# Float32r matmuls that read their tile and write their bank from the last column to the first

## The chip, the core and the metric

The kernel runs on one core of a Trainium2 chip. The metric is the device time of one execution in microseconds. The core's engines work side by side and meet at semaphores: TensorE (PE in the profile, its weight loads PEld), VectorE (DVE), ScalarE (ACT), GpSimd (POOL) and SyncE (SP, which issues most DMAs). A matmul takes a stationary operand of 128x128 and streams a moving operand of up to 512 columns past it; the product lands in one of eight banks of PSUM, with 128 rows of 512 float32 columns each.

## What is computed

One decoder layer on 256 tokens of width 2048, all in float32:

```python
h = rmsnorm(x, norm_attn_pre)
proj = h @ w_in                       # 2048 -> 4160: q, k, v of A, and c_q, c_kv, k_r of B
a_out = dilated window attention of A # 8 heads x 128, three windows merged
c_q, c_kv = rmsnorm(c_q), rmsnorm(c_kv)
q_b = c_q @ w_uq                      # 512 -> 8 x 192
kv = c_kv @ w_ukv                     # 512 -> 8 x 256
b_out = causal attention of B         # 8 heads
x = x + rmsnorm(concat(a_out, b_out) @ w_out)   # 2048 -> 2048
h = rmsnorm(x, norm_mlp_pre)
u = square(relu(h @ w_up))            # 2048 -> 8192
x = x + rmsnorm(u @ w_down)           # 8192 -> 2048
```

## The kernel before

The large products are made with float32r operands, a form of float32 that TensorE streams faster than float32 itself and rounds. To keep the precision, every operand is split in two float32r parts, `hi` (the rounded value, made by ScalarE at L306 or L310) and `lo` (what is left, made by VectorE at L307 or L311), and a product is the sum of three matmuls: hi x hi, hi x lo, lo x hi. The activations, transposed, are the stationary operand, 128 tokens at a time (`tok`), and the weights are the moving one, mostly 512 columns at a time. Of the weights' 1024-column tiles `hi` and `lo` there are eight buffers each; they are loaded on SP's queue, and partly on POOL's.

All float32r matmuls but the last 48 are issued by the helper `mm` (L295, the matmul itself is L296 in the profile); it issues the float32 matmuls of the attention too. The last 48, of the final group of `w_down`, are issued in `three_more` (L1188). Transposes are float32 and have a helper of their own (L300). The callers of `mm` are `proj` (the projections `w_in`, `w_ukv`, `w_uq` and `w_out`; its tiles have 512, 288 or 384 columns), `three` (L1016: the three matmuls of one product, used for `w_up` and `w_down`, 512 columns) and the attention heads. In `w_up` and `w_down` some blocks are multiplied with seven products in place of eight, in the manner of Strassen (`seven_products`, L1021); sums of weights and of activations are made for that on VectorE, and products are gathered in further banks (`m`, `md`).

The order of the work is written by hand. A small clock (`Flow`) in the building program adds an assumed time for each matmul, and chains of other work (evacuations, softmax, norms) are put between the matmuls when that clock says that they are due. The framework then adds the semaphores: an instruction waits for whatever wrote what it reads, or still reads what it overwrites, and also TensorE for itself, where a bank gets a new use.

Of the kernel before, what the change touches and what calls it, by code (L numbers as in the profile page):

```python
# [19 lines left out]
F32R = mybir.dt.float32r  # L20
# [243 lines left out]
def layer(nc, tc, io):  # L264
# [28 lines left out]


    def mm(out, a, b, start, stop, cost=MM):  # L295
        nc.tensor.matmul(out, a, b, start=start, stop=stop)  # L296
        flow.spend(cost)

# [160 lines left out]
    def proj(aT, chs, name, order=None, need=None, bank_of=None):  # L459
# [6 lines left out]
        for c, t, b in order:  # L466
            ch = chs[c]
            i, k0, kp = ch.tiles[t]
            ws = [weights.get(x) for x in (i if isinstance(i, list) else [i])]
            i = i if isinstance(i, list) else [i]  # L470
            if need:
                need(k0 + kp - 1, b)
            if i[0] < FINE:
                hl = [(0, 0), (1, 0)], [(0, 1)]
            else:
                hl = [(0, 0), (0, 1), (1, 0)],
            for g, passes in enumerate(hl):
                for kk in range(kp):
                    k = k0 + kk
                    for j, (o, m) in enumerate(ch.cuts):  # L480
                        wt, o = (ws[j], 0) if len(ws) > 1 else (ws[0], o)
                        for p, (x, w) in enumerate(passes):
                            mm(accs[c][b][j][:, :m], tok(aT[x], k, b), wt[w][:, kk, o:o + m],
                               k == 0 and g == 0 and p == 0,
                               k == ch.nk - 1 and g == len(hl) - 1 and p == len(passes) - 1, MM * m / 512)
                    flow.pump()
            left[c, b] -= 1
            for x in i:
                uses[x] = uses.get(x, 0) + 1
                if uses[x] == NB:  # L490
                    weights.free(x)
            if not left[c, b]:
                yield c, b, accs[c][b]
# [121 lines left out]
    def softmax_pv(wk, dl, sc, bias, scale, v, head, name):  # L615

        s = wk.tile([P, 384], F32, tag="s", bufs=2, name=f"s_{name}")
        st = wk.tile([P, 8], F32, tag="st", bufs=3, name=f"st_{name}")
        spans = ((0, 128, bias[:, 128:256]), (128, 384, bias))
        for i, (a, e, m) in enumerate(spans):  # L620
            nc.vector.tensor_tensor_reduce(
                out=s[:, a:e], in0=sc[:, a:e], in1=m, op0=OP.add, op1=OP.max, scale=1.0,
                scalar=-3e38, accum_out=st[:, i:i + 1])
        nc.vector.tensor_scalar_mul(st[:, 2:4], st[:, 0:2], -scale)
        yield dl[2]
        for i, (a, e, m) in enumerate(spans):
            nc.scalar.activation(s[:, a:e], s[:, a:e], AF.Exp, bias=st[:, 2 + i:3 + i], scale=scale,
                                 accum_out=st[:, 4 + i:5 + i])
        yield dl[3]
        nc.vector.reciprocal(st[:, 6:8], st[:, 4:6])  # L630
        for i, (a, e, m) in enumerate(spans):
            nc.vector.tensor_scalar_mul(s[:, a:e], s[:, a:e], st[:, 6 + i:7 + i])
        yield dl[4]
        tp = tp_bank(f"pT_{name}")
        for c in range(3):
            transpose(tp[:, c * P:(c + 1) * P], s[:, c * P:(c + 1) * P])
        pT = wk.tile([P, 384], F32, tag="pT", bufs=2, name=f"pT_{name}")
        nc.scalar.activation(pT, tp[:, :384], AF.Copy)
        yield dl[5]
        o = at_bank(f"o_{name}")  # L640
        mm(o[:, :S], v[0], pT[:, :S], True, False, 2 * MM)
        mm(o[:, P:S], v[1], pT[:, S:384], False, True, MM)
        split(mixT[0][:, head, :], mixT[1][:, head, :], o[:, :S])
# [407 lines left out]
    for j in range(FF // CW):  # L1051
# [9 lines left out]
        for t, b in order:  # L1061
# [19 lines left out]
            if what == "k":  # L1081
                w = weights.get(tiles[0])
# [102 lines left out]
    def three_more(out, a, w):  # L1185

        for x, z in ((0, 0), (0, 1), (1, 0)):
            nc.tensor.matmul(out, a[x], w[z], start=False, stop=(x, z) == (1, 0), skip_group_check=True)  # L1188
            flow.spend(MM)

    hp.release()
# [5 lines left out]
    for c in range(2):  # L1197
# [5 lines left out]
        for t, (what, k, tiles) in enumerate(wide_d[c]):  # L1203
# [4 lines left out]
            if what == "k":  # L1208
                w = weights.get(tiles[0])
# [37 lines left out]
    for g in (GT - 2, GT - 1):  # L1247
        for b, n in PARTS:
            for kk in range(4):
                k = 4 * g + kk  # L1250
                w = weights.get(tail[k])
                if g < GT - 1:
                    down_mm(1, us[1, g], k, b, n, w, False, kk == 3)
                else:
                    three_more(y[b][2 + n], [tok(us[1, g][x], kk, b) for x in range(2)],
                               [t[:, 0, n * 512:n * 512 + 512] for t in w])
                if (b, n) == PARTS[-1]:
                    weights.free(tail[k])
                flow.pump()
            if g < GT - 1:  # L1260
                nc.vector.tensor_tensor(out=y[b][2 + n], in0=y[b][2 + n], in1=more[b, n], op=OP.add)
                if (b, n) == (0, 0):
                    us[1, g + 1] = split_u(1, g + 1)
            elif n == 0:
                square(2, b)
                gain(2, b)
            else:
                fin = flow.start(final(b))
# [40 lines left out]
```

## Time and profile before

| | |
|---|---|
| median of 3 runs | 1047.4 us (1047.33 to 1047.88) |
| profiled execution, first to last instruction (span) | 1045.7 us |
| TensorE busy | 1035.7 us, 99% |
| VectorE, ScalarE, GpSimd busy | 80%, 60%, 5% |
| mean granted clock of TensorE | 0.997 |
| DMA | 229 MB, 219 GB/s over the span |

The profile gives the span of the execution that it took and no time of its own beside it; the median of the unprofiled runs is 1.7 us longer than this span. A busy time is the sum over an engine's instructions with overlaps counted once. Matmuls overlap in the pipeline, so a matmul's duration in a row is longer than the distance to the next one's start; that distance is read from the timeline, or from the chain that ended last, which names stretches of equal matmuls with start, length and count. In rows, `y<-hi,uhi` is output<-moving operand, stationary operand, by the program's names.

### The profile page before, as it was taken

What the parts mean: (1) busy time and instruction counts of PE and PEld (TensorE: products, weight loads), DVE (VectorE), ACT (ScalarE), POOL (GpSimd) and SP (SyncE); (2) the same over time, 40 slices, a digit from 0 to 9 for tenths busy, and PEclk for the clock granted to TensorE, in tenths of its full rate; (3) what the DMA queues carried; (4) which work ended last, traced back from release to release, by engine and by line L of the source; (5) the groups of instructions that cost most, each with busy time, mean ns of one, the idle gap of its engine ahead of it and who ended that gap; (6) DMA issues with size and microseconds to landing.
All of it is one profiled execution on the core that took longest, in us unless ns stands there. A gap on an engine that the chain in (4) does not pass through costs nothing.

```text
span 1045.7 us, 13378 instructions
## 1 busy us (share of the span) xinstructions
PE 1035.7 (99%) x4837; PEld 863.2 (83%) x4837; DVE 838.7 (80%) x1122; ACT 630.4 (60%) x848; POOL 51.5 (5%) x83
## 2 busy tenths in 40 slices
PE   9999999999999999999999999999999999999996
PEld 6888889888888888888888888888888888888885
DVE  6676536567557669999999999897899978999995
ACT  6674436565545566665765667666567564766661
POOL 0000000000000000000000000000000000111100
PEclk9999999999999999999999999999999999999998
DMA  9975547454447295646657356378778767698952
GB/s 303 370 229 148 140 129 241 146 162 153 150 156 236 92 360 188 216 147 207 202 185 246 121 201 207 113 253 325 274 276 303 265 232 261 238 332 323 356 204 83
DMA packets 79938, 229.33 MB, mean 219 GB/s; under 512 B 6912, under 2 KB 11520, under 8 KB 79488
## 3 DMA queue, kind: packets, MB, share of 16 engines
q1 hardware_dynamic: 64576, 171.47, 48.9%
q0 software_dynamic: 14864, 56.63, 15.2%
q8 instruction: 38, 0.62, 0.3%
q10 hardware_dynamic: 432, 0.37, 0.1%
q14 instruction: 28, 0.23, 0.1%
HBM read 212.72 MB, written 15.73 MB: 218 GB/s over the span
## 4 chain that ended last, share of the span: by engine, by line
PE 97%; DVE 1%; issue 1%; ACT 0%; POOL 0%; DVEq 0%; POOLq 0%; ACTq 0%
PE y L296 25%; PE acc_u L296 24%; PE acc_o L296 8%; PE m L296 7%; PE md L296 5%; PE acc_qk L296 4%; PE acc_v L296 4%; PE acc_ckv L296 2%; PE acc_ukv L296 2%; PE acc_q L296 2%; PE acc_cq L296 2%; PE acc_k L296 2%; PE acc_uq L296 2%; PE rt L300 1%; PE sc_b L296 1%
## 5 line engine op out<-in xcount | busy, mean ns | idle before, releaser
L307 DVE TENSOR_TENSOR lo<-raw,hi 128x1024 fp32r<-128x1024 f32 (+3 forms) x213 | 241.5, 1152 | 89.8 <-ACT hi L306 89.1
L306 ACT ACTIVATE hi<-raw 128x1024 fp32r<-128x1024 f32 (+3 forms) x213 | 209.9, 999 | 73.6 <-PE y L296 16.1
L296 PE MATMUL y<-hi,uhi 128*128 128x512 f32 x370 | 144.4, 390 | 0.0
L296 PE MATMUL y<-hi,ulo 128*128 128x512 f32 x370 | 144.1, 389 | 0.0
L296 PE MATMUL y<-lo,uhi 128*128 128x512 f32 x370 | 144.0, 389 | 0.0
L296 PE MATMUL acc_u<-hi,hT_hi 128*128 128x512 f32 x356 | 141.7, 398 | 0.0
L296 PE MATMUL acc_u<-hi,hT_lo 128*128 128x512 f32 x356 | 139.2, 391 | 0.4 <-DVE hT_lo L307 0.4
L296 PE MATMUL acc_u<-lo,hT_hi 128*128 128x512 f32 x356 | 138.9, 390 | 0.0
L311 DVE SCALAR_TENSOR_TENSOR lo<-raw,gcol,hi 128x1024 fp32r<-128x1024 f32 x74 | 92.5, 1279 | 9.5 <-ACT hi L310 9.5
L310 ACT ACTIVATE hi<-raw,gcol 128x1024 fp32r<-128x1024 f32 x74 | 83.7, 1148 | 25.0 <-DMA raw<-in_w_up 11.7
L296 PEld LDWEIGHTS y<-hi,ulo 128*128 128x128 f32 x370 | 69.5, 188 | 14.4
L296 PEld LDWEIGHTS y<-lo,uhi 128*128 128x128 f32 x370 | 69.5, 188 | 14.3
L296 PEld LDWEIGHTS y<-hi,uhi 128*128 128x128 f32 x370 | 69.5, 188 | 14.2
L296 PEld LDWEIGHTS acc_u<-hi,hT_lo 128*128 128x128 f32 x356 | 66.8, 188 | 14.9 <-DVE hT_lo L307 0.8
L296 PEld LDWEIGHTS acc_u<-lo,hT_hi 128*128 128x128 f32 x356 | 67.0, 188 | 12.8
L296 PEld LDWEIGHTS acc_u<-hi,hT_hi 128*128 128x128 f32 x356 | 67.0, 188 | 12.8
L306 ACT ACTIVATE hi<-u 128x1024 fp32r<-128x1024 f32 (+1 forms) x38 | 37.4, 990 | 49.2 <-DVE u L366 35.4
L307 DVE TENSOR_TENSOR lo<-st_down,hi 128x1024 fp32r<-128x1024 f32 x42 | 50.4, 1220 | 3.0 <-ACT hi L306 2.8
L296 PE MATMUL acc_o<-hi,mixT_hi 128*128 128x512 f32 x128 | 51.8, 405 | 0.0
L306 ACT ACTIVATE hi<-st_down 128x1024 fp32r<-128x1024 f32 x42 | 43.9, 1052 | 12.6 <-PE y L296 9.5
L296 PE MATMUL acc_o<-hi,mixT_lo 128*128 128x512 f32 x128 | 50.2, 392 | 0.0
L296 PE MATMUL acc_o<-lo,mixT_hi 128*128 128x512 f32 x128 | 50.0, 391 | 0.0
(328 smaller groups left out, 2087.7 us busy)
## 6 DMA issues: line engine op xcount, KB each, us to landing
raw<-in_w_down SPq DMA_DIRECT2D x86, 512.0 KB, 5.8
raw<-in_w_up SPq DMA_DIRECT2D x76, 512.0 KB, 4.6
raw<-in_w_in SPq DMA_DIRECT2D x55, 512.0 KB, 4.9
ab<-in_w_up POOLq DMA_DIRECT2D x22, 1024.0 KB, 5.4
raw<-in_w_out SPq DMA_DIRECT2D x32, 512.0 KB, 4.2
ab_down<-in_w_down POOLq DMA_DIRECT2D x11, 1024.0 KB, 7.1
ukeep<-ulo SPq DMA_DIRECT2D x15, 512.0 KB, 7.0
ulo<-ukeep POOLq DMA_DIRECT2D x15, 512.0 KB, 6.2
```

The source lines that it names most:

```text
L296: nc.tensor.matmul(out, a, b, start=start, stop=stop)
L300: nc.tensor.transpose(out, a, ident)
L306: nc.scalar.activation(hi, src, AF.Copy)
L307: nc.vector.tensor_tensor(out=lo, in0=src, in1=hi.bitcast(F32), op=OP.subtract)
L310: nc.scalar.activation(hi, src, AF.Copy, scale=g)
L311: nc.vector.scalar_tensor_tensor(out=lo, in0=src, scalar=g, in1=hi.bitcast(F32), op0=OP.mult, op1=OP.subtract)
```

## The change

Both places that issue float32r matmuls turn the moving operand and the output around in their free dimension. Column i of the weights still goes to column i of the bank. The stationary operand, float32 matmuls and transposes stay as they were.

```diff
     def mm(out, a, b, start, stop, cost=MM):
+        if b.dtype == F32R:
+            out, b = out[:, ::-1], b[:, ::-1]
         nc.tensor.matmul(out, a, b, start=start, stop=stop)
         flow.spend(cost)
...
         for x, z in ((0, 0), (0, 1), (1, 0)):
-            nc.tensor.matmul(out, a[x], w[z], start=False, stop=(x, z) == (1, 0), skip_group_check=True)
+            nc.tensor.matmul(out[:, ::-1], a[x], w[z][:, ::-1], start=False, stop=(x, z) == (1, 0), skip_group_check=True)
             flow.spend(MM)
```

In the built program the operand's pattern goes from start 0, step 1, 512 elements to start 511, step -1, 512 elements. The instructions of all engines keep their order; the lines below L295 move by two. The semaphore waits that the framework derives are not all the same. On TensorE, in the second column group of `w_up` (`acc_u` are its four banks, `rt` a bank that takes transposes of the group before), the rows before are:

```order
L296 MATMUL acc_u_00_3685<-hi_3600,hT_hi 128x512
L296 MATMUL acc_u_00_3685<-lo_3601,hT_hi 128x512 [waits DVE_49]
L296 MATMUL acc_u_00_3685<-hi_3600,hT_lo 128x512
L300 MATMUL rt_1_3750<-ident,r_1_3713 128x128 [waits Activation_49]
L300 MATMUL rt_1_3750<-ident,r_1_3713 128x128 x3
L296 MATMUL acc_u_01_3686<-hi_3600,hT_hi 128x512
```

and of the change:

```order
L298 MATMUL acc_u_00_3685<-hi_3600,hT_hi 128x512
L298 MATMUL acc_u_00_3685<-lo_3601,hT_hi 128x512 [waits DVE_49]
L298 MATMUL acc_u_00_3685<-hi_3600,hT_lo 128x512
L302 MATMUL rt_1_3750<-ident,r_1_3713 128x128 [waits PE_49,Activation_49]
L302 MATMUL rt_1_3750<-ident,r_1_3713 128x128 x3
L298 MATMUL acc_u_01_3686<-hi_3600,hT_hi 128x512
```

Nothing has moved; the first transpose into the bank also waits for TensorE's own semaphore, for a matmul 39 places earlier. On ScalarE, a little later, `hi` are splits of weights (and of their sums, `u`), `r` the evacuations of the banks `acc_u`. Before:

```order
L306 ACTIVATE hi_4054<-ab 128x1024 [waits PE_49]
L937 ACTIVATE r_0_4070<-acc_u_00_3685,rstd_pre_3344 128x512 [waits DVE_49]
L306 ACTIVATE hi_4072<-u_0_4050 128x1024 [waits DVE_49,PE_49]
L937 ACTIVATE r_0_4085<-acc_u_01_3686,rstd_pre_3344 128x512
L949 ACTIVATE uT_4092<-rt_0_4087 128x4x128 [waits PE_49]
```

and of the change:

```order
L308 ACTIVATE hi_4054<-ab 128x1024 [waits PE_49]
L939 ACTIVATE r_0_4070<-acc_u_00_3685,rstd_pre_3344 128x512 [waits DVE_49]
L308 ACTIVATE hi_4072<-u_0_4050 128x1024 [waits DVE_49]
L939 ACTIVATE r_0_4085<-acc_u_01_3686,rstd_pre_3344 128x512 [waits PE_49]
L951 ACTIVATE uT_4092<-rt_0_4087 128x4x128 [waits PE_49]
```

Here a wait for TensorE has gone from a split to the evacuation behind it, for a matmul that stands six places later. In all, TensorE's rows that wait for its own semaphore go from 50 to 92. None of the new ones is for a matmul nearer than 31 places.

## The prediction

> **What bounds the kernel now.** I read the profile's page first: the busy shares, the slices and the chain that ended last.
>
> ```profile
> span 1045.7 us, 13378 instructions
> PE 1035.7 (99%) x4837; PEld 863.2 (83%) x4837; DVE 838.7 (80%) x1122; ACT 630.4 (60%) x848; POOL 51.5 (5%) x83
> PEclk9999999999999999999999999999999999999998
> PE 97%; DVE 1%; issue 1%; ACT 0%; POOL 0%; DVEq 0%; POOLq 0%; ACTq 0%
> ```
>
> TensorE (PE) is busy for 1035.7 of 1045.7 us, it carries 97% of the chain, and the throttle grants it its clock throughout. The view of waits, cut to PE, says whether it ever waits for another engine:
>
> ```profile
> PE warm L521 <- DVE zero L518: 1.2, 1, 1.2
> PE acc_u L296 <- DVE hT_lo L307: 0.4, 1, 0.4
> PE qrt L300 <- DVE qT L772: 0.2, 1, 0.2
> ```
>
> That is all of it: 1.8 us in the run. So the time is what the matmuls themselves take, one behind the other. A busy time cannot tell that, because matmuls are pipelined: the groups give a 128x512 one a mean of 389 to 398 ns although the next starts much earlier. I take the spacing from the pieces of the chain instead, long stretches of equal matmuls with their start, length and count (the 384-column piece is from the chain of the stretch from 195 to 256 us):
>
> ```profile
> 746.46 16.32 PE y L296 x72
> 156.57 8.80 PE acc_ckv L296 x66
> 244.10 2.09 PE acc_uq L296 x12
> ```
>
> A float32r matmul with 512 moving columns takes 16.32/72 = 226.7 ns, one with 288 takes 8.80/66 = 133.3, one with 384 takes 2.09/12 = 174.2. Between 288 and 512 columns that is (226.7 - 133.3)/224 = **0.417 ns a column**, and what remains, 226.7 - 512 x 0.417, is **13.3 ns for each matmul** whatever its length (for 384 this gives 173.3, against 174.2 in the row). The change can only act on these two numbers.
>
> The program has 4083 float32r matmuls with 512 columns, 192 with 288 and 96 with 384: 4371, with 2,182,656 columns. Columns: 2,182,656 x 0.417 ns = 909 us. Fixed parts: 4371 x 13.3 ns = 58 us. So 967 of the 1045.7 us pass through the two lines that the diff touches; the rest is float32 matmuls and transposes, the start and the tail of output.
>
> **The change part by part.** It removes no instruction and moves none: on all five engines the same instructions stand in the same order. Three things differ.
>
> 1. *The tile is read in descending order.* Same columns, same count. No operand in this trace runs downwards, so the price is not shown, and I bound it. If a column in descending order costs what one in ascending order costs, the price is 0. The nearest row of a slower stream is the float32 matmul, which the trace records as two passes of an instruction:
>
> ```profile
> 228.62 0.39 PE L296 MATMUL sc_b<-kT,qT 128*128 128x128 f32 x2
> 228.84 0.39 PE L296 MATMUL sc_b<-krT,qrT 128*128 128x128 f32 x2
> 229.06 0.60 PE L296 MATMUL sc_b<-kT,qT 128*128 128x256 f32 x2
> 229.50 0.59 PE L296 MATMUL sc_b<-krT,qrT 128*128 128x256 f32 x2
> ```
>
> From 229.06 to 229.50 two passes of 256 columns take 0.44 us: 0.86 ns a column, close to twice 0.417. So a stream that moves one column where it moved two would cost 2,182,656 x (0.86 - 0.417) = 967 us more: 2014 us. The bounds of the column are 0 and +967 us. I take 0, for this reason: what streams at 0.417 here are 288, 384 and 512 columns alike, with no sign of a restart inside a tile, and a descending tile covers the same words of the same rows of memory. No row contradicts that and none proves it.
>
> 2. *The bank is written in descending order.* The same two bounds hold, as the product leaves at the rate at which columns enter. What the fixed 13.3 ns consists of, the trace does not say. It lies where one stream ends and the next begins, and that is where the order matters: the end of a tile is now column 0 and the beginning is column 511. Within a group of three products on one bank, the last column written and the first one written next are 511 columns apart, before and after. So I take 0 here too. The bounds: the fixed part may vanish (the float32 rows come near to that: 0.22 us for two 128-column passes, 0.44 for two of 256, leaves nothing fixed within the 0.01 us of the rows), which is -58 us, or be paid twice, if a stream that starts at the far end needs as much again to open: +58 us.
>
> [...]
>
> 3. *Waits.* TensorE's waits on its own semaphore go from 50 to 92: 48 new, 6 gone. For most of the new ones a separate wait instruction stands ahead of the matmul (38 of these before, 73 after). Behind such a wait the whole TensorE queue is held. But every new wait is for a matmul that stands at least 31 matmuls earlier, 31 x 0.227 = 7 us in the past, so none should find its semaphore unset. What a wait that is already met costs shows where the kernel has one now, at the first products of each seven-product step (the matmul of 500.14 and that of 502.20 carry one):
>
> ```profile
> 499.90 0.40 PE L296 MATMUL acc_u<-hi,hT_lo 128*128 128x512 f32 x1
> 500.14 0.39 PE L296 MATMUL m<-hi,hT_hi 128*128 128x512 f32 x1
> 500.36 0.39 PE L296 MATMUL m<-lo,hT_hi 128*128 128x512 f32 x1
> 501.97 0.39 PE L296 MATMUL acc_u<-hi,st 128*128 128x512 f32 x1
> 502.20 0.39 PE L296 MATMUL m<-hi,st 128*128 128x512 f32 x1
> ```
>
> The spacings are 0.24 and 0.23 us, against 0.227: nothing to 0.01 us each. For 42 net waits that is 0 to 0.4 us; I take 0.2. Should the cover of 31 matmuls fail somewhere, the price would be one drain of the pipeline, the 0.39 us of a matmul's row less its 0.23 us of spacing: 0.16 us, and 48 of them 8 us. On ScalarE six splits lose a wait for TensorE and five evacuations gain one, on VectorE five splits lose one and two instructions of the tail gain one. These engines are not waited for beyond the 0.6 us above, and the tail's two follow instructions that needed the same matmuls anyhow: 0.
>
> The sum, made against the profiled execution: 1045.7 + 0 + 0 + 0.2 = 1045.9 us of span. The median of the runs, 1047.4, lies 1.7 us above this span, so I forecast **1047.6 us**.
>
> **The rivals.**
>
> *A. The fixed part shrinks (faster).* For it: 13.3 ns is a loss that float32 passes do not show, so it belongs to how a float32r stream follows another. Against: nothing says that it has to do with direction. If it vanished, TensorE would ask for its operands sooner, and then others count:
>
> ```profile
> 0.00:100.00 100.00, 98.77 (x440) 79.42 (x441) 66.97 (x111) 63.44 (x92) 1.45 (x8) 1.00 0.82 272
> 500.00:600.00 100.00, 100.00 (x458) 82.84 (x457) 96.13 (x103) 67.23 (x79) 6.42 (x9) 1.00 0.58 190
> 900.00:1000.00 100.00, 100.00 (x443) 82.83 (x442) 95.70 (x107) 65.98 (x73) 14.86 (x25) 1.00 0.88 324
> ```
>
> The columns are the busy times of PE, PEld, DVE, ACT and POOL, then clock, DMA share and GB/s. Without the fixed part a stretch of 100 us shrinks to some 94, but VectorE needs 96 in two of them, and the first stretch is bound by transfers in part (share 0.82). I take off 6 us for that: 1047.6 - 58 + 6, about **995 us** in full, and anything between that and no change in part. [...]
>
> *B. Half rate (much slower).* One mechanism: reads or bank writes take two neighbouring columns at once, and only in ascending pairs, so that a descending stream moves one column where it moved two. Place: inside each of the 4371 matmuls. For it: float32r moves four bytes a column twice as fast as a float32 pass does, so something is done in pairs or at double width. Against: a pair taken from above lies in the same words. Price as worked out above: **2014 us**. It decides from the first column on; nothing hides it, since TensorE is already 97% of the chain.
>
> *C. The fixed part grows (slower).* One mechanism: opening a stream at its far end takes longer, between each two matmuls. At the full second 13.3 ns it gives 1047.6 + 58 = **1106 us**. It decides early: a measurement of this kernel can tell about 0.2% (2.1 us) from no change, and 2.1 us over 4371 matmuls is 0.48 ns, little more than the time of one column. For it: no matmul here has any slack. Against: the same as in A.
>
> *D. The change does not arrive*: as tile and bank are turned together, the product is the same, and a lowering could turn both back. The program still has the step of -1 in both operands, so this has little for it, and it would give 1047.4, within the forecast.
>
> **How the numbers follow.** No change (with D): 0.36. A: 0.22. C: 0.22. B and anything beyond C: 0.20. The no-change case alone would lie between 1045.5 and 1049.7. The range has to reach both A and C, so it runs from 995 to 1106; it leaves out only B, with its 2 in 10. I keep no change as the single likeliest because the two bounds of the fixed part lie equally far on both sides of it, and because the column's lower bound is the one with a reason. Faster by over 0.2%: 0.22; within: 0.36; slower: 0.42.
>
> **What would show it.** For the sum: the pieces of the chain again give 226.7, 133.3 and 174 ns, and the matmuls' operands show a step of -1. For A or C: spacings of 288 and 512 columns move by the same number of nanoseconds. For B: the difference between them changes, from 0.417 ns a column towards 0.86. For the waits: no new row for PE in the view of waits, and no matmul behind a new wait more than 0.01 us late. In A, VectorE's busy time in the stretch from 500 to 600 us would fill it, and PE would wait for `lo`. My forecast is wrong if either of the two numbers, 0.417 or 13.3, depends on direction; I have no row that excludes it.

## The result, and the profile after

The change makes the kernel slower: 1072.47 us (median of 4 runs, 1072.12 to 1073.34) against 1047.45 (4 runs), a ratio of 1.0239 with a 95% interval of 1.0225 to 1.0252. That is 25.0 us. In the profiled executions the span goes from 1045.7 to 1070.3 us, 24.6 more, at mean granted clocks of 0.997 and 0.998. From the page of the changed kernel:

```profile
span 1070.3 us, 13409 instructions
PE 1060.0 (99%) x4837; PEld 865.3 (81%) x4837; DVE 839.4 (78%) x1122; ACT 631.3 (59%) x848; POOL 50.2 (5%) x83
PE 96%; DVE 1%; issue 1%; DMA 0%; ACT 0%; SPq 0%; POOL 0%; DVEq 0%; POOLq 0%; ACTq 0%
```

TensorE's busy time has grown by 24.3 us, VectorE's and ScalarE's by less than 1. The 31 instructions more are separate waits: 35 more on TensorE, 4 fewer on ScalarE. What TensorE waits for, from the view of waits:

```profile
PE warm L523 <- DVE zero L520: 1.2, 1, 1.2
PE acc_qk L298 <- ACT hi L308: 0.5, 1, 0.5
PE acc_u L298 <- DVE hT_lo L309: 0.3, 1, 0.3
```

2.0 us in all, against 1.8: no new wait of any size. So the matmuls follow each other more slowly. The pieces of the chain (start, length, count), again one for each length of the moving tile; the last is from the chain of the stretch from 195 to 262 us:

```profile
762.53 16.80 PE y L298 x72
160.04 8.80 PE acc_ckv L298 x66
248.53 2.14 PE acc_uq L298 x12
```

With 512 columns a matmul now takes 16.80/72 = 233.3 ns, 6.7 more. With 288 it takes 133.3 as before. With 384 it takes 178.3 against 174.2, 4.1 more. The loss depends on the length, and not in proportion.

The sum of it: 4083 x 6.67 ns = 27.2 us, and 96 x 4.1 ns = 0.4 us: 27.6, some 3 us more than the spans differ by. Most of these 3 us are hidden behind transposes, where the next matmuls were spaced more widely before. In `w_up`, from the start of one group of four transposes to the next, with six 512-column matmuls between them, before:

```profile
454.46 0.60 PE L300 MATMUL rt<-ident,r 128*128 128x128 f32 x4
456.29 0.60 PE L300 MATMUL rt<-ident,r 128*128 128x128 f32 x4
```

and after:

```profile
463.06 0.60 PE L302 MATMUL rt<-ident,r 128*128 128x128 f32 x4
464.90 0.60 PE L302 MATMUL rt<-ident,r 128*128 128x128 f32 x4
```

1.83 us became 1.84, where six times 6.7 ns would be 0.04. The second and third matmul behind the transposes were spaced 0.23 to 0.24 us already. By the starts in the two traces, the 621 spacings of 512-column matmuls that begin within eleven places behind a transpose or a float32 matmul grew by 1.6 us together, where 6.7 ns each would be 4.1: that is 2.5 of the 3 us.

### The profile page after: what moved, and what is told of

Its sections match the earlier page's. It is cut to its first block, busy times and chain, and to the rows that moved or that the text cites. A ratio compares the mean times of both kernels' runs of the same rounds, so it can differ in the third digit from the quotient of the medians.

```text
span 1070.3 us, 13409 instructions
## 1 busy us (share of the span) xinstructions
PE 1060.0 (99%) x4837; PEld 865.3 (81%) x4837; DVE 839.4 (78%) x1122; ACT 631.3 (59%) x848; POOL 50.2 (5%) x83
## 4 chain that ended last, share of the span: by engine, by line
PE 96%; DVE 1%; issue 1%; DMA 0%; ACT 0%; SPq 0%; POOL 0%; DVEq 0%; POOLq 0%; ACTq 0%
PE y L298 26%; PE acc_u L298 24%; PE acc_o L298 8%; PE m L298 7%; PE md L298 5%; PE acc_v L298 4%; PE acc_qk L298 4%; PE acc_ckv L298 2%; PE acc_ukv L298 2%; PE acc_q L298 2%; PE acc_cq L298 2%; PE acc_k L298 2%; PE acc_uq L298 2%; PE rt L302 1%; PE sc_b L298 1%
## 5 line engine op out<-in xcount | busy, mean ns | idle before, releaser
L298 PE MATMUL y<-hi,uhi 128*128 128x512 f32 x370 | 147.5, 399 | 0.0
L298 PE MATMUL y<-hi,ulo 128*128 128x512 f32 x370 | 147.1, 398 | 0.0
L298 PE MATMUL y<-lo,uhi 128*128 128x512 f32 x370 | 147.1, 398 | 0.0
L298 PE MATMUL acc_u<-hi,hT_hi 128*128 128x512 f32 x356 | 144.4, 406 | 0.0
L298 PE MATMUL acc_u<-hi,hT_lo 128*128 128x512 f32 x356 | 141.7, 398 | 0.3 <-DVE hT_lo L309 0.3
L298 PE MATMUL acc_u<-lo,hT_hi 128*128 128x512 f32 x356 | 141.5, 398 | 0.0
```

## The experiments

**Read alone, write alone, and every second one.** Three kernels take the change apart. The first turns the moving tile only, in `mm` as shown and likewise in `three_more`:

```diff
     def mm(out, a, b, start, stop, cost=MM):
+        if b.dtype == F32R:
+            b = b[:, ::-1]
```

> Only the moving tile is read from its last column to its first, in every float32r matmul; the bank is written in ascending order, so each piece of up to 512 output columns comes out mirrored and the output is not the layer's. TensorE has its 50 waits on itself, as before the change. If the descending READ makes the loss: 512-column matmuls 233.3 ns apart, 1072 us. If the descending WRITE makes it: 226.7 ns and 1047 us. If the 42 added waits make it: 226.7 ns and 1047 us. If it takes both together (a mismatch of neither): 1047 us here and in the write-only kernel.

The second turns the bank only, in both places:

```diff
     def mm(out, a, b, start, stop, cost=MM):
+        if b.dtype == F32R:
+            out = out[:, ::-1]
```

> Only the bank is written from its last column to its first, in every float32r matmul; the moving tile is read in ascending order, so the columns come out mirrored and the output is not the layer's. TensorE has the 92 waits of the change. If the descending WRITE makes the loss: 512-column matmuls 233.3 ns apart, 1072 us. If the descending READ makes it: 226.7 ns and 1047 us. If the added waits make it: 1072 us, but with the loss at single matmuls behind a wait and the median spacing still 226.7 ns.

The third turns both, in every second matmul (and in the middle one of each product of `three_more`):

```diff
     def mm(out, a, b, start, stop, cost=MM):
+        if b.dtype == F32R:
+            turn["down"] = not turn.get("down", True)
+            if turn["down"]:
+                out, b = out[:, ::-1], b[:, ::-1]
```

> Every second float32r matmul runs downwards (tile and bank together), the others upwards; the output is the layer's. If each descending stream pays on its own: the mean spacing of 512-column matmuls is 230.0 ns, half of the loss, 1060 us. If it is the step from the end of one stream to the start of the next that costs (column 511 to 0, or 0 to 511), that step vanishes here, and the time falls to 1047 us or below it. If every change of direction costs something of its own: above 1060 us.

Measured, with 1047.88 us for the kernel before beside them: the read alone 1071.71 us, ratio to before 1.0222 (1.0205 to 1.0239); the write alone 1047.72, ratio 0.9998 (0.9989 to 1.0008); to and fro 1058.46, ratio 1.0096 (1.0081 to 1.0111). One row of the chain's pieces from each kernel, the same place of `w_up`, 42 matmuls; reading down first:

```profile
579.41 9.80 PE acc_u L298 x42
```

writing down:

```profile
568.15 9.52 PE acc_u L298 x42
```

and to and fro:

```profile
572.93 9.66 PE acc_u L300 x42
```

These are 233.3, 226.7 and 230.0 ns. **The read makes the whole loss** as far as the intervals tell (1.0222 against the change's 1.0239, and they overlap), and the write none. The write-only kernel has all 92 of the change's waits and runs as fast as before, so the waits cost nothing either. With every second stream descending, the spacing of this piece is half way, and the time rises by 10.6 us, somewhat less than half of the 23.8 of the read alone. Each descending stream pays on its own. That can be read from the starts in the traces: for matmuls of 512 columns that stand between two others of 512, the mean distance to the next start is 227.7 ns before and 233.9 after the change, and in this kernel 228.0 behind an ascending matmul and 233.4 behind a descending one. The step from where one stream ends to where the next begins is gone in that kernel, and nothing is faster than before for it.

**Streams alone.** A kernel that computes nothing of the layer (it copies x to the output) runs streams of 24 matmuls, each kind by itself, with the moving tile's type, start, length and direction, and the bank's direction, as the differences.

```diff
+    for n in (512, 480, 448, 416, 384, 352, 320, 288, 256):
+        stream("up", "r", n, 1, 1)
+        stream("down", "r", n, -1, -1)
+        stream("rddown", "r", n, -1, 1)
+        stream("wrdown", "r", n, 1, -1)
+        stream("fro", "r", n, 0, 0)
...
```

> None of the layer is computed (x is copied to the output): streams of 24 float32r matmuls with 512, 480, 448, 416, 384, 352, 320, 288 and 256 columns, each up, down, with only the read down, only the write down, and to and fro; then bf16 with 512 and 256 columns, float32 with 256, 512-column float32r tiles that start 1, 4, 16, 32 and 512 columns into their buffer, 288 columns at the end of a bank, and one stationary operand kept. If a fixed part of each descending matmul grew, all lengths lose the same 6.7 ns. If a descending stream loses a little at each block of columns, the loss goes with the length (6.7 ns at 512, 5.0 at 384, 3.3 at 256). If the loss is what is not hidden behind a fixed slack of about 300 columns, it is 0 up to some length and then grows: 0 at 288, 4.4 at 384, 6.7 at 512. bf16 and float32 should show no loss if only the four-byte stream at full rate is short of reads, and the same loss if the write is what is slow.

These are from one profiled execution. Its pieces of the chain, in the order of the program: 512 columns up, down, read down, write down, to and fro; 384 up and down; 320 up and down; 288 up and down; bf16 (`bup`, `bdown`) with 512 up and down, then with 256; and 512 columns that start 4 columns into the buffer, up and down (`offupg`, `offdownh`):

```profile
14.26 5.47 PE up L45 x24
19.73 5.61 PE down L45 x24
25.33 5.60 PE rddown L45 x24
30.93 5.46 PE wrdown L45 x24
36.39 5.67 PE fro L45 x24
...
115.70 4.16 PE up L45 x24
119.86 4.26 PE down L45 x24
...
156.28 3.52 PE up L45 x24
159.80 3.52 PE down L45 x24
...
173.97 3.16 PE up L45 x24
177.12 3.20 PE down L45 x24
...
204.51 4.91 PE bup L45 x22
209.43 5.18 PE bdown L45 x24
214.61 2.62 PE bup L45 x24
217.23 2.62 PE bdown L45 x24
...
238.09 5.55 PE offupg L45 x24
243.64 5.60 PE offdownh L45 x24
```

Divided by 24, down less up is 5.8 ns at 512 columns, 4.2 at 384, 0 at 320 and 1.7 at 288. (The ascending stream of 512 starts slowly here; from its fifth spacing on the starts give 226.9 ns up and 233.3 down, close to the layer's 6.7.) The lengths between give 2.5 (480), 4.2 (448), 2.9 (416) and 1.3 (352), and at 256 columns down is 0.8 ns faster. So the loss is not one fixed part for all lengths, nor in proportion to the length. It is near zero up to some 350 columns and uneven above; "a fixed slack, then growth" is the nearest of the three expectations, but not by a clean line. bf16 loses nothing at 512 columns, where float32r does: 5.18 us down, and 5.20 up from the stream's first start at 204.23 (one of its 24 matmuls has no record), so 216 and 217 ns. At 256 columns bf16 (2.62 us) and float32 (3.46 us for 16 passes) are the same both ways, but there float32r loses nothing either; float32 with longer tiles was not run. The to-and-fro stream here, 236.3 ns, is slower than the stream that only goes down, though in the layer the same alternation cost about half; here one tile is read over and over, in the layer three matmuls use two tiles in turn. Why stays open.

**What unit has to ascend.** A second kernel of that kind keeps 512 columns, and varies the stationary operand's width and the order in which the moving tile's blocks are read; the bank is always written upwards.

```diff
+    for tag, i in (("two", 2), ("four", 4), ("eight", 8), ("sixteen", 16), ("thirtytwo", 32), ("onetwentyeight", 128)):
+        stream(tag + "blocksdown", 512, lambda t: t[:, 0:512].rearrange("p (g i) -> p g i", i=i)[:, ::-1, :])
+        stream(tag + "insidedown", 512, lambda t: t[:, 0:512].rearrange("p (g i) -> p g i", i=i)[:, :, ::-1])
...
```

> None of the layer is computed (x is copied to the output): streams of 24 float32r matmuls with 512 columns, up and down, with 128, 64 and 32 stationary columns; blocks of 2, 4, 8, 16, 32 and 128 columns taken in descending order with ascending columns inside, and blocks in ascending order with descending columns inside; 256 columns at steps of 1, 2, -2 and 4; and tiles that start 2, 8, 64, 128 and 256 columns into their buffer. Theory 1, the fetch takes neighbouring columns together and only in ascending pairs: descending inside blocks costs 233.3 ns at every block size, blocks in descending order cost 226.7 from size 2 on. Theory 2, the fetch takes lines of 4 columns (or larger blocks) and looks ahead upwards: blocks of 2 and 4 in descending order cost 233.3, large ones less and less, and descending inside blocks of 2 and 4 costs 226.7. Theory 3, the fixed 13.3 ns and the loss are both the next stationary operand's load taking turns at the moving tile's reads: with 64 stationary columns both halve (6.7 ns and 3.3 ns over the 213.3 of the columns, so 220 up and 223 down), with 32 both quarter. If the fixed part does not belong to the load, 226.7 and 233.3 with 128, 64 and 32 alike. A step of 2 keeps two of four columns of a line: 120 ns for 256 columns if that is enough, as at step 1; a step of 4 up to twice as much.

The pieces of the chain, again from one profiled execution. `half` and `quart` have 64 and 32 stationary columns, `inside` rows descend inside each block and have the blocks ascending, the four step rows have 256 columns, and the last three ascend from a start 8, 64 and 128 columns into the buffer:

```profile
24.32 5.52 PE halfup L45 x24
29.84 5.60 PE halfdown L45 x24
35.45 5.56 PE quartup L45 x24
41.01 5.60 PE quartdown L45 x24
46.61 5.60 PE twoblocksdown L45 x24
52.21 5.46 PE twoinsidedown L45 x24
57.67 5.61 PE fourblocksdown L45 x24
63.28 5.46 PE fourinsidedown L45 x24
68.74 5.61 PE eightblocksdown L45 x24
74.34 5.59 PE eightinsidedown L45 x24
79.94 5.60 PE sixteenblocksdown L45 x24
85.54 6.40 PE sixteeninsidedown L45 x24
91.94 5.58 PE thirtytwoblocksdown L45 x24
97.53 5.68 PE thirtytwoinsidedown L45 x24
103.21 5.46 PE onetwentyeightblocksdown L45 x24
108.67 5.61 PE onetwentyeightinsidedown L45 x24
114.28 2.87 PE stepone L45 x24
117.15 5.44 PE steptwo L45 x24
122.59 5.60 PE steptwodown L45 x24
128.19 5.60 PE stepfour L45 x24
...
145.04 5.60 PE eightoffup L45 x24
...
156.25 5.49 PE sixtyfouroffup L45 x24
...
167.34 5.46 PE onetwentyeightoffup L45 x24
```

Theory 3 falls: it wanted 220 and 223 ns with 64 stationary columns, and no narrower operand makes a stream faster by more than 0.01 us. Down stays at 5.60 us, while up grows from 5.47 (128 stationary columns, above) to 5.52 and 5.56; so the difference shrinks, but because the ascending stream gets slower. Why it does stays open. Theory 1 falls: descending inside blocks of 2 or 4 is free (5.46), and blocks of 2 in descending order cost everything (5.60). What Theory 2 forecast came: inside four columns, 16 bytes, the two orders that were tried cost nothing (5.46), and **the order of these groups of four** counts. Descending inside blocks of 8, which swaps every two groups, costs the whole loss (5.59). Blocks of 4, 8, 16 cost the whole loss when they descend (5.60 to 5.61), blocks of 32 nearly all of it (5.58), blocks of 128 nothing (5.46).

The order is not all that counts. An ascending stream that starts 8 columns into the buffer, two whole groups, is as slow as a descending one (5.60); from 64 it is nearly as fast as from 0 (5.49), and from 128 as fast (5.46). In the streams before, starts of 1, 4, 16 and 32 columns gave 5.67, 5.55, 5.50 and 5.58. No theory here forecast that. It makes a rival: a descending stream begins at column 511, so it might be slow for where it begins and not for its order. Two rows speak against this. Descending from a start of 4, the first group read is that of columns 512 to 515; an ascending stream that begins at column 512 is fast (5.46), and this one takes 5.60. (It does not settle the matter, as that same tile is slow upwards too, 5.55.) And descending inside blocks of 16 takes 6.40, more than any start costs by itself (at most 5.67), so the order inside a stream does count. For the plain descending stream the rival is made unlikely and not excluded.

**The same in the layer.** Three kernels compute the whole layer with such patterns in tile and bank. `three_more` has the same pattern as `mm` in each. The first, with `i = 4`, descends inside each group of four:

```diff
     def mm(out, a, b, start, stop, cost=MM):
+        if b.dtype == F32R:
+            out, b = [t.rearrange("p (g i) -> p g i", i=4)[:, :, ::-1] for t in (out, b)]
```

> The whole layer; in every float32r matmul the groups of four columns go upwards, and the four inside each go downwards, in tile and bank alike (every column is still paired with its own). If the loss comes from the order of 16-byte groups and not from the direction inside them, as the streams alone suggest: 512 columns at 226.7 ns, 1047.5 us. If any descending step costs: 1072 us. If the three-dimensional pattern itself costs: above 1047.5 here and in the next two alike.

The second lets the groups descend:

```diff
+            out, b = [t.rearrange("p (g i) -> p g i", i=4)[:, ::-1, :] for t in (out, b)]
```

> The whole layer; groups of four columns go downwards and the four inside each go upwards. By the order of groups: 233.3 ns and 1072 us, the whole loss of the change although three of four steps are upwards. By the number of descending steps (a quarter): 1053 us.

The third lets blocks of 128 descend:

```diff
+        if b.dtype == F32R and b.shape[-1] % 128 == 0:
+            out, b = [t.rearrange("p (g i) -> p g i", i=128)[:, ::-1, :] for t in (out, b)]
```

> The whole layer; in float32r matmuls of 512 and 384 columns blocks of 128 columns go downwards, and inside a block all goes upwards: every stream starts near the far end of the tile and of the bank and ends near column 127. If it were the start at the far end that opens a stream slowly (rival C as it was put): 1072 us. If it is the repeated step back to an earlier group, of which there are three here in place of 127: 1047.5 to 1050 us (the stream alone had 227.2 ns).

Measured, with 1047.99 us for the kernel before beside them: 1048.06 us, ratio 1.0001 (0.9991 to 1.0010); 1072.38, ratio 1.0227 (1.0210 to 1.0244); 1047.84, ratio 0.9998 (0.9989 to 1.0008). The same piece of `w_up` in each, descending inside four:

```profile
570.04 9.52 PE acc_u L298 x42
```

groups of four descending:

```profile
580.09 9.80 PE acc_u L298 x42
```

and blocks of 128 descending:

```profile
568.98 9.52 PE acc_u L298 x42
```

All three came out as the order of groups says. They do not decide against the rival: their streams begin at columns 3, 508 and 384, and by the start alone the first and the last would be fast and the second slow as well. None of these versions is faster than the kernel before, and no stream of 512 float32r columns is faster than its 226.7 ns.

## Why the forecast of no change was wrong

**What bounds the kernel** was right. TensorE alone sets the time (99% busy, 96% of the chain), so 6.7 ns on 4083 matmuls went into the end almost undiminished, 25 of 27.6 us.

**Step 1, the read, is the step that failed.** I took 0 because "a descending tile covers the same words of the same rows of memory". It does, but reading it downwards costs a float32r stream something all the same, most likely by the order in which groups of four columns are asked for (1072.38 us with the groups descending, 1048.06 with only the columns inside them). It costs 6.7 ns on a matmul of 512 columns, or 3%, the time of 16 columns at 0.417 ns; my upper bound for this term was twice the time. The prediction held the rate per column and the fixed part apart, and expected that one or the other would move. Neither moved by itself: 288 columns lose nothing, 384 lose 4.1 ns and 512 lose 6.7, which no fixed part and no price per column gives. The signs that I had set down say the same: 288 and 512 columns did not move together, as A or C would have it, and the difference between them rose only from 0.417 to 0.446 ns a column, far from B's 0.86. That 1072 us lies within the range of 995 to 1106 is luck: the upper end was C's price, and C's mechanism is not what happened.

**Step 2, the write**, at 0, was right: the write-only kernel measures 0.9998. A bank written downwards (9.52 us for 42 matmuls, 226.7 ns), or in groups of four downwards inside (9.52 us, ratio 1.0001), showed no loss here.

**Step 3, the waits**, at 0.2 us, was right within what can be told: the write-only kernel has the 92 waits and is as fast as before.

**Rival C** had the right sign, and about two fifths of its full price of 58 us. Its mechanism, a stream that opens slowly at the far end, is refuted. The kernel with blocks of 128 opens every 512-column stream at column 384 and writes there first, and loses nothing (ratio 0.9998); the stream that descends inside blocks of 128 opens at column 127 and loses all (5.61 us). **Rival B** (half rate) did not come: a pair taken from above (descending inside blocks of 2, 5.46 us) is as good as one from below (5.47), as the argument against it said. The streams with a step of 2, in which no two wanted columns are neighbours, take 5.44 us in place of 2.87 for 256 columns, close to twice. **Rival A** had no support: no float32r matmul of 512 columns came out faster than 226.7 ns. **Rival D** falls with the loss itself.

What stays open is what happens inside the fetch. Three steps back (blocks of 128, 5.46 us) cost nothing, 15 (blocks of 32, 5.58) cost nearly as much as 127 (groups of four, 5.61), and the price depends unevenly on the length. The lines and the look-ahead of Theory 2 are my guess: the rows show times, no run shows what is fetched together or ahead, and the guess explains neither the ascending streams that start 1 to 32 columns off nor the blocks of 16 that descend inside (6.40 us). Nor do the runs say what the fixed 13.3 ns of a float32r matmul is; a narrower stationary operand does not make it smaller (5.52 and 5.56 us against 5.47).

## What to carry to other kernels

Let the moving operand of a float32r matmul of 512 columns ascend in memory (226.7 ns against 233.3 here), from a start of 0, 128, 256 or 512 columns in its buffer (5.46 to 5.48 us for 24; the seven starts from 1 to 64 that were tried took 5.49 to 5.67). Inside 16 bytes, and with whole blocks of 128 columns, the orders that were tried cost the layer nothing (1048.06 and 1047.84 us against 1047.99). If a layout has to be turned around, do it on the side of PSUM: the bank written downwards cost nothing here (1047.72 us against 1047.88). And when the busiest engine has next to no idle time (2.0 us of waits here), a few nanoseconds per instruction are the whole result (6.7 ns on 4083 matmuls, 25.0 us), so read the spacing of starts for every length of tile and not for one.

## What the runs showed of the hardware that was not expected

- At 512 columns float32r is sensitive to the direction of the read (5.47 us up, 5.60 with the read down) and bf16 is not (5.20 us up, 5.18 down, with tile and bank turned together).
- An ascending float32r tile of 512 columns that starts 8 columns into its buffer takes 5.60/24 = 233.3 ns, as a descending one does; from 128 it has no loss.
- Descending inside blocks of 16 columns, with the blocks ascending, is worse than descending throughout: 6.40/24 = 266.7 ns against 233.3. Inside blocks of 8 it is 233, inside blocks of 32 237, inside blocks of 128 234. No theory above gives the 266.7.
- A float32r tile read at a step of 2 takes nearly twice the time (5.44 against 2.87 us for 24 matmuls of 256 columns: 226.7 ns each, not 120), and a step of 4 little more than that (5.60).
